# A load buffer more in the two MLPs of a decoder trunk, paid for with smaller operand tiles

## The chip, the cores and the metric

One NeuronCore of a Trainium2 chip runs the whole program. It has TensorE (matrix products), VectorE, ScalarE, GpSimd (its queue is called POOL here) and SyncE (SP), which only issues DMAs. The metric is the device time of one execution in microseconds.

## The reference, cut to what matters

Two pre-norm residual layers over 256 positions of width 2048. The mixers (attention of four kinds) stay as they are here. The change lies in the MLP that follows each mixer, with 8192 hidden columns:

```python
def squared_relu_mlp(h, w_up, w_down):
    return jnp.square(jax.nn.relu(h @ w_up)) @ w_down

for layer in range(DEPTH):                      # DEPTH = 2
    ...                                         # x = x + mixer(rms_norm(x))
    h = rms_norm(x, mlp_norm[layer])
    x = x + squared_relu_mlp(h, w_up[layer], w_down[layer])
```

All is float32; `w_up` and `w_down` are 64 MB each per layer, and every weight is read from memory once.

## The kernel before, in words

**Split operands.** Every float32 operand is split into a high part in TensorE's reduced format (`hi`) and the remainder (`lo`), and a product is made of hi·hi, hi·lo and lo·hi. For the weights this is done on the fly: a load brings 1 MB into a tile `raw` of 128 × 2048 (8 KB a partition), ScalarE copies 1024 columns of it into `hi` (L1317), VectorE subtracts to give `lo` (L1328), and TensorE uses both.

**One stream.** The whole kernel is a list `stream` of chunks (1024 weight columns a partition each), in the order in which TensorE consumes them. Chunks belong to load units (`Unit`), one DMA each on SP's queue. The main loop at the end of `trunk` makes, for chunk `i`, the `hi` of the chunks up to `i + 5` (`hi_to`, five buffers), the `lo` of those up to `i + 4` (`lo_to`, four buffers), and then the matmuls of chunk `i` (`chunk`). When the last chunk of a unit has its `lo`, `load_to` issues the next load. There are three `raw` buffers (`RAW_BUFS`), so a load waits until the unit three before it has been read.

**The MLP.** The hidden columns are cut into eight groups of 1024. `up_list(grp)` makes the group's hidden values in four blocks `b` of 256 columns (16 matmul steps each, into one PSUM pair called `up` or `s`); `up_done` evicts a block (ScalarE `t` L1002, VectorE L1003, ScalarE L1004 and L1008 into `hr`) and a job turns `hr` into the operand tile `hs`. For the first six groups the second matrix is applied with a fast scheme for 2 × 2 blocks (seven products in place of eight), for which `hs` holds seven combinations, each as hi and lo: a tile of 7 × 256. The pair `b = 3`, the one listed in `PLAIN`, goes the plain way with eight products and fills only four rows of its tile. `product_list(grp)` covers the output columns in four column blocks `cb`, with two load units of `w_down` each; `prep13` and `prep24` (L1062 to L1070) make the weights' combinations `w13` and `w24`. Products of group `grp` and up blocks of group `grp + 1` are interleaved by a fixed pattern in `mlp`: two chunks of products, one of up, and so on, so that a column block's seven chunks go with four chunks of up, and the loads come as w_down, w_up, w_down, w_up.

At the end of a column block ScalarE copies the two halves of its sums into `stage` tiles (L1118, two buffers), and POOL's queue stores them to `sums` in DRAM: the first group plainly (L1121), the others with an adding DMA (L1123). After the last of the six groups `combine` makes the outputs from `sums` by further adding DMAs (L1135) and copies (L1140), while TensorE goes on with the up blocks of the last group and then with the second matrix for the last two groups in the ordinary way ("down" blocks).

**Pools.** Each mixer and each MLP opens a memory pool of its own when its first chunk is reached and closes it when the next begins (`open_pool`, `pool_ctx.close`); the pools of successive phases use the same memory. The `raw`, `hi` and `lo` buffers are in a pool of their own (`wts`) that lasts throughout. The first five units go to tiles borrowed from the first mixer (`early`).

Of the kernel before, what the change touches and what calls it, by code (L numbers as in the profile page):

```python
# [10 lines left out]
F32 = mybir.dt.float32  # L11
F32R = mybir.dt.float32r
# [5 lines left out]
P = 128  # L18
# [20 lines left out]
RAW_BUFS, HI_BUFS, LO_BUFS = 3, 5, 4  # L39
# [6 lines left out]
class Jobs:  # L46


    def __init__(self, budget):
        self.t, self.budget = 0, budget  # L50
        self.jobs, self.done, self.owner = [], set(), {}
# [16 lines left out]
    def need(self, key):  # L68
        rounds = 0
        while key not in self.done:  # L70
            last = self.owner[key]
            for job in list(self.jobs):
                if job in self.jobs and not job[3]:
                    self.step(job)
                if key in self.done or job is last and rounds < 8:
                    break
            rounds += 1
# [33 lines left out]
class Unit:  # L111


    def __init__(self, load):
        self.load, self.users, self.raw = load, 0, None


class Chunk:
# [20 lines left out]
def trunk(ctx, tc, x, attn_norm, mlp_norm, w_up, w_down, ev_w_in, ev_q_norm, ev_w_uq, ev_kv_norm,  # L139
          ev_w_ukv, ev_w_out, od_w_in, od_sinks, od_w_out, final_norm, c_perm, c_rope, c_dist, out):  # L140
    nc = tc.nc
    wts = ctx.enter_context(tc.tile_pool(name="wts", bufs=1))
# [13 lines left out]
    def f32(ap):  # L156
        return ap.bitcast(F32)
# [4 lines left out]
    def temp():  # L162
        return tmp.tile([P, 2, T], F32, name="t", bufs=3)

    def split_into(dst, src, scale=1.0):

        act(dst[:, :, 0:T], src, AF.Copy, scale=scale)
        tt(dst[:, :, T:], src, f32(dst[:, :, 0:T]), op=OP.subtract)
# [3 lines left out]
    xin, early = [], []  # L172
# [21 lines left out]
    st = {}  # L194

    def open_banks(pool_ctx, name):
        st["banks"] = pool_ctx.enter_context(
            tc.tile_pool(name=name, bufs=1, space=bass.MemoryType.PSUM, reuse_waits="tile"))
# [228 lines left out]
    stream = []  # L427
# [535 lines left out]
    def mlp(layer, last):  # L963
# [4 lines left out]
        E = {}  # L968

        def open_pool():  # L970
            open_banks(pool_ctx, f"mlp{layer}_ps")
            E["pool"] = pool_ctx.enter_context(tc.tile_pool(name=f"mlp{layer}", bufs=1, reuse_waits="tile"))

        def load_gain():
            fn = [E["pool"].tile([P, D // 2], F32, name=n) for n in ("w13", "w24")]
            for i in range(2):
                c = slice(i * D // 2, (i + 1) * D // 2)
                nc.gpsimd.dma_start(fn[i], final_norm[c].unsqueeze(0).to_broadcast([P, D // 2]))
            E["fn"] = lambda c0, n: fn[c0 // (D // 2)][:, c0 % (D // 2):c0 % (D // 2) + n]

        NGRP, NS = 8, 6
        PLAIN = (3,)
        W = FF // NGRP
        nb = W // T
        up, down = w_up[layer], w_down[layer]
        sums = [dram.tile([P, 8 * T], F32, name=f"sums{layer}_{cb}") for cb in range(4)]
        hs = {}
# [11 lines left out]
        def up_done(grp, b):  # L999
            def f(ps):  # L1000
                t = temp()
                act(t, ps[:, :, T:], AF.Copy)  # L1002
                tt(t, ps[:, :, 0:T], t, op=OP.add)  # L1003
                act(t, t, AF.Relu)  # L1004
                if (grp, b) != (0, 0):
                    need(("h", layer) + ((grp, b - 1) if b else (grp - 1, nb - 1)))
                r = E["pool"].tile([P, 8, P], F32, name="hr", bufs=1)
                act(r[:, 0:4].rearrange("p (j k) t -> p j (k t)", j=2), t, AF.Square)  # L1008

                def job():  # L1010
                    h = E["pool"].tile([P, 7, 2 * P], F32R, name="hs", bufs=2 * nb)
                    if grp >= NS:
                        h = h.rearrange("p o t -> p (o t)")[:, 0:4 * T].rearrange("p (j t) -> p j t", j=2)
                        split_into(h, r[:, 0:4].rearrange("p (j k) t -> p j (k t)", j=2))
                    elif b in PLAIN:
                        act(h[:, 0:4, 0:P], r[:, 0:4], AF.Copy)
                        yield 1, 0
                        tt(h[:, 0:4, P:], r[:, 0:4], f32(h[:, 0:4, 0:P]), op=OP.subtract)
                    else:

                        tt(r[:, 4], r[:, 0], r[:, 2], op=OP.add)
                        tt(r[:, 6], r[:, 1], r[:, 0], op=OP.subtract)
                        tt(r[:, 5], r[:, 4], r[:, 1], op=OP.subtract)
                        tt(r[:, 7], r[:, 3], r[:, 5], op=OP.subtract)
                        yield 1, 0
                        act(h[:, :, 0:P], r[:, 1:8], AF.Copy)
                        yield 1, 0
                        tt(h[:, :, P:], r[:, 1:8], f32(h[:, :, 0:P]), op=OP.subtract)
                    hs[grp, b] = h
                    jobs.done.add(("h", layer, grp, b))  # L1030
                    yield 1, 0
                jobs.spawn(job(), keys=[("h", layer, grp, b)], delay=1)
            return f

# [166 lines left out]
        for grp in range(NS):  # L1201
            s, u = product_list(grp), up_list(grp + 1)
            for i in range(len(u)):
                a, b = (i // 4 * 7 + (0, 2, 4, 5, 7)[i % 4 + e] for e in range(2))
# [10 lines left out]
        for b in range(8):  # L1215
# [3 lines left out]
            else:  # L1219
                add(Block("T", w, h_mov, down_done(b), take=take_free(b), extra=add_sums(b)))  # L1220
        return open_pool, pool_ctx.close


# [63 lines left out]
    for f in (even_mixer, lambda: mlp(0, False), odd_mixer, lambda: mlp(1, True)):  # L1287
        a = len(stream)
        phases.append((a,) + tuple(f()))
    starts = {p[0]: i for i, p in enumerate(phases)}  # L1290
    total = len(stream)
    his, los = {}, {}
    units = []
    for block, c in stream:
        if block.chunks[c].unit not in units[-2:]:
            units.append(block.chunks[c].unit)
    at = {"load": 0, "free": 0, "hi": 0, "lo": 0}

    def load_to(n):
        while at["load"] < min(n, len(units)):  # L1300
            unit = units[at["load"]]
            n = at["load"]
            unit.raw = early[n] if n < len(early) else wts.tile([P, 2048], F32, name="raw", bufs=RAW_BUFS)
            unit.load(unit.raw)
            at["load"] += 1

    def views(i, dst):
        block, c = stream[i]
        chunk = block.chunks[c]
        return chunk.views(chunk.unit.raw, dst)  # L1310

    def hi_to(n):
        while at["hi"] < min(n, total):
            i = at["hi"]
            his[i] = wts.tile([P, 1024], F32R, name="hi", bufs=HI_BUFS)
            for d, r in views(i, his[i]):
                act(d, r, AF.Copy)  # L1317
            prep = stream[i][0].chunks[stream[i][1]].prep
            if prep:
                prep()  # L1320
            at["hi"] += 1

    def lo_to(n):
        while at["lo"] < min(n, total):
            i = at["lo"]
            los[i] = wts.tile([P, 1024], F32R, name="lo", bufs=LO_BUFS)
            for (d, r), (h, _) in zip(views(i, los[i]), views(i, his[i])):
                tt(d, r, f32(h), op=OP.subtract)  # L1328
            at["lo"] += 1
            unit = stream[i][0].chunks[stream[i][1]].unit  # L1330
            unit.users -= 1
            if unit.users == 0:
                at["free"] += 1
                load_to(max(at["free"], len(early)) + RAW_BUFS)

    def split_to(n):
        hi_to(n)
        lo_to(n)

    def chunk(i):  # L1340
        block, c = stream[i]
        consume(block, c, his.pop(i), los.pop(i))
# [49 lines left out]
    for b, n in enumerate((1, 2, 3, 3, 5, 5, 6, 6)):  # L1392
        load_x(b)
        load_to(n)
    load_to(7)
    x_turn(0)
    gains(g_first, 16, 0)
# [27 lines left out]
    for i in range(START, total):  # L1425
        if i in starts:
            phases[starts[i] - 1][2]()
            phases[starts[i]][1]()
        hi_to(i + HI_BUFS)
        lo_to(i + LO_BUFS)  # L1430
        chunk(i)
        block, c = stream[i]
        if block.tiles * len(block.chunks[c].kts) == 8 or block.kind == "S" and c in (1, 3, 4, 6):
            jobs.tick()
# [44 lines left out]
```

## Time and profile before

| | |
|---|---|
| median of three runs | 2197.22 us (2196.88 to 2203.35) |
| the profiled execution | 2204.07 us, of which the span of its instructions is 2202.3 us |
| TensorE matmul busy | 2159.3 us, 98% of the span |
| VectorE, ScalarE, POOL busy | 1588.7, 1284.6, 162.6 us |
| mean granted TensorE clock | 0.996 |
| DMA traffic | 459.43 MB, 209 GB/s over the span |
| loads of `w_up` | 128 of 1024 KB, 5.8 us from issue to landing in the median |

The page gives busy times and shares over the whole span, a chain of waits, groups of instructions and DMA issues; answers of the trace give single stretches. `L1317` is line 1317 of the kernel. "Idle before" an instruction is time in which its engine did nothing, and the name behind the arrow is what ended it. The first MLP occupies about 360 to 1090 us of the span, the second about 1460 us to the end.

### The profile page before, as it was taken

The page shows a single profiled execution, that of the slowest core. Times are in us where ns is not written, and L with a number is a line of the kernel's source. Part 1 is how long each engine was busy: PE and PEld are TensorE (multiplying, and loading weights), DVE is VectorE, ACT ScalarE, POOL GpSimd, SP SyncE. Part 2 cuts the span into 40 slices and gives each one's busy share as a digit, 9 for nine tenths or more (in the row PEclk, how much of TensorE's full clock was granted, in tenths as well). Part 3 has the DMA queues.
Part 4 walks back from the last instruction along what each step waited for, and adds up shares of the span by engine and source line. Part 5 has one row for each costly group of instructions (what it writes and reads, how often), then busy time and mean ns, then how long its engine had stood idle before and what let it go on. Part 6 is the DMA issues. An engine that isn't in the chain of part 4 may idle for free.

```text
span 2202.3 us, 35006 instructions
## 1 busy us (share of the span) xinstructions
PE 2159.3 (98%) x14038; PEld 1953.4 (89%) x14038; DVE 1588.7 (72%) x2120; ACT 1284.6 (58%) x1777; POOL 162.6 (7%) x217
## 2 busy tenths in 40 slices
PE   9999999999999999999999999999999999999998
PEld 7898988999999889878888889889999898988887
DVE  6765666788888778747766665567887887876476
ACT  6554545667666666555545446456766666665552
POOL 0000000000000000321000000000000000003210
PEclk9999999999999999999999999999999999999999
DMA  8545456578888879897654456566878888888973
GB/s 261 178 149 163 149 177 191 191 246 233 240 238 238 235 217 250 233 271 213 195 172 137 153 172 183 147 186 195 263 222 242 226 243 234 238 241 219 284 208 112
DMA packets 313811, 459.43 MB, mean 209 GB/s; under 512 B 11864, under 2 KB 198304, under 8 KB 313648
## 3 DMA queue, kind: packets, MB, share of 16 engines
q1 hardware_dynamic: 288416, 392.32, 56.5%
q0 software_dynamic: 25200, 64.86, 15.0%
q8 instruction: 110, 1.80, 0.3%
q14 instruction: 53, 0.43, 0.1%
q10 hardware_dynamic: 32, 0.01, 0.0%
HBM read 404.73 MB, written 60.82 MB: 211 GB/s over the span
## 4 chain that ended last, share of the span: by engine, by line
PE 58%; issue 22%; DMA 13%; DVE 3%; POOL 2%; ACT 2%; SPq 0%; POOLq 0%; ACTq 0%; DVEq 0%
PE mm L472 14%; PE mm L473 8%; DMA raw<-w_up 7%; PE s L472 6%; DMA sums<-sums 5%; PE up L472 5%; PE s L473 3%; PE up L473 3%; DVE lo L1328 2%; PE s L493 2%; PE s L494 2%; PE s L495 2%; PE mm L461 2%; PE mm L463 2%; PE mm L462 2%
## 5 line engine op out<-in xcount | busy, mean ns | idle before, releaser
L1328 DVE TENSOR_TENSOR lo<-raw,hi 128x1024 fp32r<-128x1024 f32 (+2 forms) x804 | 851.2, 1082 | 269.0 <-ACT hi L1317 109.3
L1317 ACT ACTIVATE hi<-raw 128x1024 fp32r<-128x1024 f32 (+2 forms) x804 | 738.9, 942 | 506.5 <-DMA raw<-w_up 185.3
L472 PE MATMUL up<-xs,hi 128*128 128x512 f32 x1440 | 522.6, 399 | 11.1 <-DVE t L1003 6.9
L473 PE MATMUL up<-xs,lo 128*128 128x256 f32 x1536 | 428.1, 284 | 9.4 <-DVE lo L1328 8.2
L494 PE MATMUL s<-lo,hs 128*128 128x256 f32 x1392 | 390.6, 281 | 0.0
L493 PE MATMUL s<-hi,hs 128*128 128x256 f32 x1392 | 390.5, 281 | 0.0
L495 PE MATMUL s<-hi,hs 128*128 128x256 f32 x1392 | 390.3, 280 | 0.0
L472 PEld LDWEIGHTS up<-xs,hi 128*128 128x128 f32 x1440 | 271.8, 189 | 70.9 <-DVE t L1003 10.4
L472 PE MATMUL mm<-xs,hi 128*128 128x512 f32 x885 | 319.4, 401 | 0.0
L473 PEld LDWEIGHTS up<-xs,lo 128*128 128x128 f32 x1536 | 290.5, 189 | 22.2 <-DVE lo L1328 19.6
L493 PEld LDWEIGHTS s<-hi,hs 128*128 128x128 f32 x1392 | 262.3, 188 | 6.5
L494 PEld LDWEIGHTS s<-lo,hs 128*128 128x128 f32 x1392 | 261.8, 188 | 2.1
L495 PEld LDWEIGHTS s<-hi,hs 128*128 128x128 f32 x1392 | 262.4, 188 | 0.0
L473 PE MATMUL mm<-xs,lo 128*128 128x256 f32 x944 | 259.1, 280 | 0.2 <-DVE lo L1328 0.2
L1328 DVE TENSOR_TENSOR lo<-w,hi 128x1024 fp32r<-128x1024 f32 x144 | 175.7, 1220 | 56.7 <-ACT hi L1317 56.7
L472 PEld LDWEIGHTS mm<-xs,hi 128*128 128x128 f32 x885 | 166.0, 188 | 37.3
L473 PEld LDWEIGHTS mm<-xs,lo 128*128 128x128 f32 x944 | 177.3, 188 | 3.1 <-DVE lo L1328 0.5
L472 PE MATMUL s<-xs,hi 128*128 128x512 f32 x480 | 171.5, 398 | 8.3 <-ACT stage L1118 5.6
L1317 ACT ACTIVATE hi<-w 128x1024 fp32r<-128x1024 f32 x144 | 150.9, 1048 | 19.2 <-DVE w L1070 15.8
L472 PE MATMUL s<-hs,hi 128*128 128x512 f32 x450 | 161.0, 398 | 0.0
L473 PE MATMUL s<-xs,lo 128*128 128x256 f32 x512 | 141.5, 281 | 1.2 <-DVE lo L1328 1.2
L1118 ACT ACTIVATE stage<-s 128x1024 f32<-128x1024 f32 x96 | 97.8, 1018 | 58.6 <-PE s L495 56.4
(312 smaller groups left out, 3130.6 us busy)
## 6 DMA issues: line engine op xcount, KB each, us to landing
raw<-w_up SPq DMA_DIRECT2D x128, 1024.0 KB, 5.8
raw<-w_down SPq DMA_DIRECT2D x128, 1024.0 KB, 5.5
sums<-stage POOLq DMA_DIRECT2D x96, 512.0 KB, 8.5
raw<-od_w_in SPq DMA_DIRECT2D x36, 1024.0 KB, 5.1
raw<-ev_w_in SPq DMA_DIRECT2D x30, 1024.0 KB, 5.3
raw<-ev_w_out SPq DMA_DIRECT2D x16, 1024.0 KB, 5.1
raw<-od_w_in SPq DMA_DIRECT2D x20, 512.0 KB, 4.9
sums<-sums POOLq DMA_DIRECT2D x64, 128.0 KB, 7.0
```

The lines of the kernel that those rows point to most:

```text
L461: mm(o, xh, hi[:, n], start=first, stop=False)
L462: mm(o, xh, lo[:, n], start=False, stop=False)
L463: mm(o, xl, hi[:, n], start=False, stop=last)
L472: mm(ps[:, j], hi[:, n, c], m, start=first, stop=False)
L473: mm(ps[:, j, 0:T], lo[:, n, c], m[:, 0:T], start=False, stop=False)
L493: mm(ps, x[:, a, 0:P], hi[:, w], start=(i, o) == bank[0], stop=False)
L494: mm(ps, x[:, a, 0:P], lo[:, w], start=False, stop=False)
L495: mm(ps, x[:, a, P:], hi[:, w], start=False, stop=(i, o) == bank[-1])
L1118: act(stage, ps.rearrange("p b c -> p (b c)"), AF.Copy)
L1317: act(d, r, AF.Copy)
L1328: tt(d, r, f32(h), op=OP.subtract)
```

## The change

Two things are done together. While an MLP runs, a fourth load buffer `raw` is taken from the MLP's own pool. The three buffers in `wts` become three tokens `None` in a list `spare`, and the fourth is a token with the number of its phase, added when the MLP's pool has been opened; every load takes the first token of the list, every unit that has been read gives its token back at the end of the list, and a token of a phase that the next unit no longer belongs to is thrown away. The fourth buffer takes 8 KB a partition. The operand tiles of the pair in `PLAIN` get a name and a size of their own (`hp`, 4 × 256 in place of 7 × 256, two tiles), and six tiles `hs` are left of eight, which is 6 KB a partition less.

```diff
 class Unit:
     def __init__(self, load):
-        self.load, self.users, self.raw = load, 0, None
+        self.load, self.users, self.raw, self.slot = load, 0, None, "early"
...
         def open_pool():
             open_banks(pool_ctx, f"mlp{layer}_ps")
             E["pool"] = pool_ctx.enter_context(tc.tile_pool(name=f"mlp{layer}", bufs=1, reuse_waits="tile"))
+            st["own_raw"] = lambda: E["pool"].tile([P, 2048], F32, name="raw")
...
                 def job():
-                    h = E["pool"].tile([P, 7, 2 * P], F32R, name="hs", bufs=2 * nb)
+                    if b in PLAIN:
+                        h = E["pool"].tile([P, 4, 2 * P], F32R, name="hp", bufs=2 * len(PLAIN))
+                    else:
+                        h = E["pool"].tile([P, 7, 2 * P], F32R, name="hs", bufs=2 * (nb - len(PLAIN)))
...
-    for block, c in stream:
-        if block.chunks[c].unit not in units[-2:]:
-            units.append(block.chunks[c].unit)
-    at = {"load": 0, "free": 0, "hi": 0, "lo": 0}
+    for i, (block, c) in enumerate(stream):
+        unit = block.chunks[c].unit
+        if unit not in units[-2:]:
+            unit.phase = sum(a <= i for a in starts) - 1
+            units.append(unit)
+    at = {"load": 0, "hi": 0, "lo": 0}
+
+    spare = [None] * RAW_BUFS
 
     def load_to(n):
         while at["load"] < min(n, len(units)):
             unit = units[at["load"]]
-            n = at["load"]
-            unit.raw = early[n] if n < len(early) else wts.tile([P, 2048], F32, name="raw", bufs=RAW_BUFS)
+            n_early = at["load"] < len(early)
+            if not n_early:
+                if spare and spare[0] not in (None, unit.phase):
+                    spare.pop(0)
+                if not spare:
+                    return
+                unit.slot = spare.pop(0)
+            if n_early:
+                unit.raw = early[at["load"]]
+            elif unit.slot is None:
+                unit.raw = wts.tile([P, 2048], F32, name="raw", bufs=RAW_BUFS)
+            else:
+                unit.raw = st["own_raw"]()
             unit.load(unit.raw)
             at["load"] += 1
...
             if unit.users == 0:
-                at["free"] += 1
-                load_to(max(at["free"], len(early)) + RAW_BUFS)
+                if unit.slot != "early":
+                    spare.append(unit.slot)
+                load_to(len(units))
...
         if i in starts:
             phases[starts[i] - 1][2]()
+            st.pop("own_raw", None)
             phases[starts[i]][1]()
+            if "own_raw" in st:
+                spare.append(starts[i])
+                load_to(len(units))
```

## The prediction

> **What bounds the kernel now.** I read the page first, then the waits of TensorE, of ScalarE and of the load queue, then three timelines, then the windows. Page, parts 1 and 6:
>
> ```profile
> span 2202.3 us, 35006 instructions
> ...
> PE 2159.3 (98%) x14038; PEld 1953.4 (89%) x14038; DVE 1588.7 (72%) x2120; ACT 1284.6 (58%) x1777; POOL 162.6 (7%) x217
> ...
> raw<-w_up SPq DMA_DIRECT2D x128, 1024.0 KB, 5.8
> ...
> sums<-stage POOLq DMA_DIRECT2D x96, 512.0 KB, 8.5
> ```
>
> TensorE is the bound: no other engine comes near 98%. A load buffer takes no matmul away, so all that can be won is time in which TensorE stands still or runs slowly. Its idle time seems to be only 2202.3 − 2159.3 = 43 us, start and end included; but the page says that matmul ends are modelled, so a stop shorter than one matmul hides in "busy". I therefore measure the loss by the beat of the work. In the MLPs every column block of the second matrix (`cb`, four a group, six groups) ends with the same two issues to `sums` on POOL's queue. Timeline of POOL, first issue of each column block (first MLP, then the second):
>
> ```profile
> 425.52 0.59 POOL L1121 DMA_DIRECT2D sums<-stage  x1 [331.75 <-ACT stage L1118]
> ...
> 511.77 0.90 POOL L1123 DMA_DIRECT2D sums<-stage  x1 [19.18 <-ACT stage L1118]
> ...
> 533.33 0.86 POOL L1123 DMA_DIRECT2D sums<-stage  x1 [18.83 <-ACT stage L1118]
> ...
> 643.81 0.86 POOL L1123 DMA_DIRECT2D sums<-stage  x1 [18.52 <-ACT stage L1118]
> ...
> 666.52 0.86 POOL L1123 DMA_DIRECT2D sums<-stage  x1 [18.18 <-ACT stage L1118]
> ...
> 869.39 0.86 POOL L1123 DMA_DIRECT2D sums<-stage  x1 [18.33 <-ACT stage L1118]
> ...
> 1524.10 0.59 POOL L1121 DMA_DIRECT2D sums<-stage  x1 [427.90 <-ACT stage L1118]
> ...
> 1966.62 0.86 POOL L1123 DMA_DIRECT2D sums<-stage  x1 [18.25 <-ACT stage L1118]
> ```
>
> From 425.52 to 511.77 lie four column blocks: 86.25 / 4 = 21.56 us each, and 511.77 to 533.33 is 21.56 again. That is the beat when nothing is late. From 643.81 to 666.52 it is 22.71. The twenty blocks from 425.52 to 869.39 take 443.87 us where 20 × 21.56 = 431.2 would do: 12.7 us lost. The twenty from 1524.10 to 1966.62 take 442.52: 11.3 us lost. Together 24.0.
>
> Who is late? Waits of TensorE, of ScalarE and VectorE, and of the load queue (SPq):
>
> ```profile
> PE up L473 <- DVE lo L1328: 8.2, 9, 3.3
> PE up L472 <- DVE t L1003: 6.9, 14, 1.0
> PE s L472 <- ACT stage L1118: 5.6, 2, 4.2
> PE up L472 <- ACT hi L1317: 4.1, 2, 2.7
> ...
> ACT hi L1317 <- DMA raw<-w_up: 185.3, 75, 11.0
> DVE lo L1328 <- ACT hi L1317: 167.2, 115, 9.9
> ...
> SPq L1179 <- DVE lo L1328: 727.9, 160, 11.8
> SPq L1041 <- DVE lo L1328: 587.1, 96, 10.7
> ```
>
> TensorE waits for what VectorE and ScalarE make; those wait for `hi`; `hi` waits 185.3 us for loads of `w_up`; and the queue that issues the MLP loads waits 727.9 + 587.1 us for `lo` to have read a buffer. So these loads are late because they start late, for want of a buffer.
>
> **The change, part by part.** *The buffer.* Four loads are made per column block. Timeline of the load queue over one beat, and two of these loads in the chain of waits (start, duration):
>
> ```profile
> 655.58 0.37 SPq L1041 DMA_DIRECT2D raw<-w_down  x1
> 662.47 0.37 SPq L1179 DMA_DIRECT2D raw<-w_up  x1
> 666.00 0.37 SPq L1041 DMA_DIRECT2D raw<-w_down  x1
> 669.06 0.37 SPq L1179 DMA_DIRECT2D raw<-w_up  x1
> 677.47 0.37 SPq L1041 DMA_DIRECT2D raw<-w_down  x1
> 684.09 0.37 SPq L1179 DMA_DIRECT2D raw<-w_up  x1
> 687.62 0.37 SPq L1041 DMA_DIRECT2D raw<-w_down  x1
> ...
> 662.47 5.48 DMA raw<-w_up
> ...
> 690.69 10.76 DMA raw<-w_up
> ```
>
> With three buffers a buffer's turn is from one load to the third after it: 655.58 to 669.06, 662.47 to 677.47, 666.00 to 684.09, 669.06 to 687.62, or 13.5, 15.0, 18.1, 18.6, mean 16.3. The beat allows 21.56 × 3/4 = 16.2. The turn just fails, which is why the first MLP holds the beat for some blocks and then falls behind as its reserve is used up. With four buffers the beat allows 21.56: 5.3 us of room in each turn. Each load is issued at the release before its own (the one of 662.47 at 655.58, that of 669.06 at 666.00), on average 21.56/4 = 5.4 us earlier.
>
> What the lateness does in one beat, ScalarE's timeline:
>
> ```profile
> 668.03 1.06 ACT L1317 ACTIVATE hi<-raw 128x1024 fp32r<-128x1024 f32 x1 [1.80 <-DMA raw<-w_up]
> 669.00 1.01 ACT L1118 ACTIVATE stage<-s 128x1024 f32<-128x1024 f32 x1
> 669.90 1.05 ACT L1317 ACTIVATE hi<-w 128x1024 fp32r<-128x1024 f32 x1
> 670.85 0.59 ACT L1002 ACTIVATE t<-up 128x512 f32<-128x512 f32 x1
> ```
>
> ScalarE stands 1.80 us before a `hi` whose load (662.47 + 5.48) has just landed; the two evictions queued behind it, `stage` and `t`, go late, and TensorE cannot start the next up block in their one bank. The 14 waits on `t` are thus mostly the load's as well. A load 5.4 us earlier covers 1.80. A window in which the beat held (length, then busy time of PE, PEld, DVE, ACT, POOL, then TensorE's granted clock, DMA share, GB/s):
>
> ```profile
> 500.00:550.00 50.00, 50.00 (x351) 46.59 (x350) 41.46 (x56) 34.13 (x42) 3.49 (x4) 1.00 0.84 232
> ```
>
> Next late after that is nothing that I can find: the same instructions ran here in the same order with TensorE busy throughout and VectorE at 41.46 of 50 us. I take 22 of the 24.0 us; ends 0 (the load is not the cause) and 24.0.
>
> *The change of groups.* After the last products, the `combine` copies on POOL's queue and the loads share the DMA engines. Windows, same columns:
>
> ```profile
> 900.00:950.00 50.00, 44.76 (x290) 40.23 (x289) 27.50 (x32) 22.08 (x28) 14.04 (x19) 0.97 0.92 237
> 950.00:1000.00 50.00, 48.23 (x271) 41.42 (x272) 29.79 (x30) 32.56 (x42) 17.18 (x23) 1.00 1.02 269
> 2000.00:2050.00 50.00, 41.21 (x255) 36.72 (x254) 26.46 (x31) 23.34 (x29) 15.76 (x22) 0.93 0.90 230
> ...
> 915.00:920.00 5.00, 3.79 (x13) 3.30 (x14) 4.97 (x7) 4.20 (x5) 1.65 (x2) 0.66 0.78 145
> ...
> 2025.00:2030.00 5.00, 4.92 (x37) 4.42 (x36) 4.72 (x7) 3.57 (x6) 3.30 (x5) 1.00 0.40 49
> 2030.00:2040.00 10.00, 10.00 (x74) 9.43 (x73) 4.56 (x6) 2.01 (x2) 3.23 (x5) 1.00 1.00 211
> ```
>
> Idle here: 5.24 + 1.77 + 8.79 = 15.8 us. The clock costs 0.03 × 50 + 0.07 × 50 = 5.0 more. Together 20.8. Before the worst stop the DMA engines stand at 0.40 (2025 to 2030: all three buffers are full) and then run at 1.00 without catching up; a fourth buffer would have used that hole. But inside the crowd an earlier issue only waits longer. Ends: 0, if the crowd decides, and 20.8, if the earlier start does. I take half, 10, since one hole stands against one crowded stretch.
>
> At 915 to 920, right after TensorE's longest wait on `lo` (3.3 us), the clock is at 0.66. The Trainium skill, TensorE: Matmul & The Clock Gate, Part 1: The HAM clock gate, says that an idle window of about 3.4 us sends the clock to half rate, and that shorter gaps don't. By that rule halving the stops would bring back all of the 5.0, and the gain here would be 7.9 + 5.0 = 12.9 and not 10; the trace shows the drop, not how short a stop must be to avoid it.
>
> *The room.* The operand tile of the fourth pair goes from `hs` (7 rows) to `hp` (4 rows), two tiles of it and six of `hs` in place of eight. Each turn stays two groups long, the same instructions write and read the same elements, so no wait is added: 0, covered by the beat at 21.56, which held with the same turn. If a turn did shorten, the next group's `act` into it would stop ScalarE; nothing in the code does that.
>
> *The start of each MLP.* One more load goes out when the pool opens. It is queued on SP behind loads already issued; what waits behind it is only the next load, which needs a release some microseconds later. Its memory is that of the mixer's first tiles, last read in the attention, before the output projection. 0; if it had to wait for the projection's end, one load would be late by a few microseconds, once per MLP, within the range.
>
> *The rule for issuing.* Outside the MLPs `load_to` has the same three tokens in the same order: 0. When units of the next mixer come up the fourth token is dropped: 0.
>
> Sum: 22 + 10 = 32 us. The profiled execution took 2204.07 (span 2202.3 and 1.8 around it): 2172. The median of the three runs shown is 2197.22, 6.85 lower. If those 6.85 are fewer stops, only 44.8 − 6.9 = 38 us are there to win and the share of 32/44.8 gives 27: 2170; if not, 2197 − 32 = 2165. I say 2168.
>
> **Rivals.**
> 1. *The DMA engines decide.* For it: shares of 1.00 at 2030 and 1.02 at 950. Against it in the products: 0.84 at full beat. Then the group changes win nothing and the products half to all of theirs: 12 to 24 us, 2173 to 2185. The Trainium skill, DMA: Bandwidth & Descriptors, Queues, rings and completion order, says that each DMA engine takes turns between the queues that have work, packet by packet; so a second load waiting in the same queue gets no larger share beside POOL's copies. The trace does not show the turns themselves.
> 2. *The load is not the cause, or the buffer comes to nothing.* If ScalarE's order (`stage`, `hi`, `t`) makes the stops by itself, TensorE's waits on `t` stay, and the fourth load only sits longer. Against it: the five beats from 425.52 to 533.33 ran in that order without loss. Gain 0 to 6: 2191 to 2197.
> 3. *Slower: POOL's stores starve.* `stage` has two buffers; each must be stored before its next use, 21.56 us later. The store takes 8.5 us in the median; it would have to pass 19.7 (beat less the issue of 0.86 and the eviction of 1.01) to decide. Each microsecond above costs TensorE one, in up to 40 blocks: at 20.7 us some 40 us, 2237. Loads ask for the same bytes per beat as before, which speaks against it.
>
> **How the numbers follow.** Forecast (both terms in good part, 2152 to 2175): 0.68. Rival 1: 0.20. Rival 2: 0.07. Rival 3: 0.05. The lower end takes the whole pool, 2197 − 45 = 2152; the upper must reach into rival 1 and past it until at most 2 in 10 is out: 2188. A measurement here tells 0.3%, 6.6 us, from no change. Forecast and rival 1 are faster by more than that: 0.88; rival 2 within it: 0.07; rival 3 slower: 0.05.
>
> **What would show it.** Right: the POOL issues at 21.56 us through all six groups; ScalarE's wait on `raw<-w_up` from 185.3 to under 60; loads landing later after their issue than 5.8 us, as two are under way; the windows of the group change at a clock of 1.00. Wrong: beats of 22 and more with `hi` waiting for loads issued long before (rival 1), or with no such wait (rival 2); `stage` waiting for `sums` (rival 3).

## The result, and the profile after

The changed kernel takes 2162.59 us in the median (2159.46 to 2164.85) against 2198.73 (2196.88 to 2203.35) of the kernel before in the same comparison: 36.1 us less, a ratio of 0.9832 with a 95% interval of 0.9811 to 0.9852. Compared once more, beside the last experiments, it was 0.9820 (0.9801 to 0.9840). The forecast was 2168, in a range of 2152 to 2188.

The page of the kernel after, parts 1 and 6:

```profile
span 2160.3 us, 35009 instructions
...
PE 2141.6 (99%) x14038; PEld 1949.6 (90%) x14038; DVE 1588.6 (74%) x2120; ACT 1290.0 (60%) x1777; POOL 163.1 (8%) x217
...
raw<-w_up SPq DMA_DIRECT2D x128, 1024.0 KB, 5.6
```

The span is 42.0 us shorter than before; the profiled execution of before (2204.07) lay above its timed runs, which is the difference to 36.1. VectorE and ScalarE are busy about as long as before (1588.6 and 1290.0 us) in a shorter span.

POOL's timeline, first store of a column block (`sums<-stage`; L1121 and L1123 have become L1125 and L1127):

```profile
425.72 0.59 POOL L1125 DMA_DIRECT2D sums<-stage  x1 [331.42 <-ACT stage L1122]
...
641.31 0.87 POOL L1127 DMA_DIRECT2D sums<-stage  x1 [18.83 <-ACT stage L1122]
...
662.87 0.86 POOL L1127 DMA_DIRECT2D sums<-stage  x1 [18.83 <-ACT stage L1122]
...
856.91 0.86 POOL L1127 DMA_DIRECT2D sums<-stage  x1 [18.83 <-ACT stage L1122]
...
1503.51 0.59 POOL L1125 DMA_DIRECT2D sums<-stage  x1 [428.63 <-ACT stage L1122]
...
1934.70 0.86 POOL L1127 DMA_DIRECT2D sums<-stage  x1 [18.84 <-ACT stage L1122]
```

Twenty blocks take 856.91 − 425.72 = 431.19 us in the first MLP and 1934.70 − 1503.51 = 431.19 in the second: the beat of 21.56 throughout (641.31 to 662.87 as well, where it was 22.71). That is 12.7 and 11.3 us less than before, 24.0 together. The other 18.0 of the 42.0 lie behind these blocks.

Waits of the kernel after, of ScalarE and TensorE:

```profile
ACT stage L1122 <- DMA sums<-stage: 13.8, 4, 6.0
...
PE s L472 <- ACT stage L1122: 3.8, 2, 2.1
...
ACT hi L1336 <- DMA raw<-w_up: 1.7, 3, 1.1
```

ScalarE's wait for loads of `w_up` has gone from 185.3 us to 1.7. Beside 1.6 us at the start of the second MLP, as before, TensorE has two stops left in the MLPs, and they have another cause: a `stage` tile whose store has not landed. ScalarE's timeline and the windows show the place (columns as in the prediction's windows):

```profile
925.14 1.03 ACT L1122 ACTIVATE stage<-s 128x1024 f32<-128x1024 f32 x1 [5.68 <-DMA sums<-stage]
...
2003.28 1.03 ACT L1122 ACTIVATE stage<-s 128x1024 f32<-128x1024 f32 x1 [6.04 <-DMA sums<-stage]
```

```profile
900.00:950.00 50.00, 48.27 (x303) 43.12 (x302) 29.07 (x31) 30.95 (x38) 14.52 (x20) 1.00 0.98 264
950.00:1000.00 50.00, 50.00 (x290) 43.68 (x290) 32.32 (x39) 28.59 (x37) 14.21 (x20) 1.00 0.95 252
...
2000.00:2050.00 50.00, 47.91 (x265) 41.45 (x264) 25.19 (x25) 29.41 (x36) 16.80 (x24) 0.97 1.05 290
```

The idle time in these three windows is 1.73 + 0 + 2.09 = 3.8 us, where it was 15.8, and the lowered clock costs 0.03 × 50 = 1.5 us, where it was 5.0. That is 15.5 of the 18.0; the rest is not located.

### The profile page after: what moved, and what is told of

Same layout as the page of the kernel before. It is cut to its first block, busy times and chain, and to the rows that moved or that the text cites. A ratio compares the mean times of both kernels' runs of the same rounds, so it can differ in the third digit from the quotient of the medians.

```text
span 2160.3 us, 35009 instructions
## 1 busy us (share of the span) xinstructions
PE 2141.6 (99%) x14038; PEld 1949.6 (90%) x14038; DVE 1588.6 (74%) x2120; ACT 1290.0 (60%) x1777; POOL 163.1 (8%) x217
## 4 chain that ended last, share of the span: by engine, by line
PE 49%; issue 39%; DMA 8%; POOL 4%; ACT 0%; POOLq 0%; SPq 0%; DVE 0%; ACTq 0%
PE mm L472 15%; PE mm L473 8%; PE s L472 6%; DMA sums<-sums 6%; PE s L473 4%; POOL sums L1127 3%; PE mm L461 2%; PE mm L463 2%; PE mm L462 2%; PE up L472 1%; DMA sums<-stage 1%; PE mm L475 1%; PE side L352 1%; PE up L473 1%; PE s L495 1%
## 5 line engine op out<-in xcount | busy, mean ns | idle before, releaser
L472 PE MATMUL up<-xs,hi 128*128 128x512 f32 x1440 | 516.6, 396 | 0.0
L473 PE MATMUL up<-xs,lo 128*128 128x256 f32 x1536 | 423.5, 281 | 0.0
L494 PE MATMUL s<-lo,hs 128*128 128x256 f32 x1008 | 282.9, 281 | 0.0
L493 PE MATMUL s<-hi,hs 128*128 128x256 f32 x1008 | 282.9, 281 | 0.0
L495 PE MATMUL s<-hi,hs 128*128 128x256 f32 x1008 | 282.7, 280 | 0.0
L493 PEld LDWEIGHTS s<-hi,hs 128*128 128x128 f32 x1008 | 189.9, 188 | 6.5
L494 PEld LDWEIGHTS s<-lo,hs 128*128 128x128 f32 x1008 | 189.7, 188 | 2.1
L495 PEld LDWEIGHTS s<-hi,hs 128*128 128x128 f32 x1008 | 190.0, 189 | 0.0
L472 PE MATMUL s<-hs,hi 128*128 128x512 f32 x360 | 129.9, 399 | 0.0
```

The costliest lines, as they stand in the source:

```text
L472: mm(ps[:, j], hi[:, n, c], m, start=first, stop=False)
L473: mm(ps[:, j, 0:T], lo[:, n, c], m[:, 0:T], start=False, stop=False)
L493: mm(ps, x[:, a, 0:P], hi[:, w], start=(i, o) == bank[0], stop=False)
L494: mm(ps, x[:, a, 0:P], lo[:, w], start=False, stop=False)
L495: mm(ps, x[:, a, P:], hi[:, w], start=False, stop=(i, o) == bank[-1])
```

## The experiments

The theory at the start was the prediction's: with three buffers a buffer's turn (load plus hold) is a little too long for the beat. The rivals: the new layout of the tiles does it; any reserve of 8 KB would do; the DMA engines decide.

### The smaller operand tiles alone

```diff
-                    h = E["pool"].tile([P, 7, 2 * P], F32R, name="hs", bufs=2 * nb)
+                    if b in PLAIN:
+                        h = E["pool"].tile([P, 4, 2 * P], F32R, name="hp", bufs=2 * len(PLAIN))
+                    else:
+                        h = E["pool"].tile([P, 7, 2 * P], F32R, name="hs", bufs=2 * (nb - len(PLAIN)))
```

> The smaller operand tiles (hp and hs) alone, with three load buffers as before. Theory (the fourth buffer makes the whole gain): the same time as before, 2198.7 within 6 us, and beats of the column blocks that lose 10 to 13 us over twenty blocks in each MLP, as before. Rival (the new layout of the operand tiles or of the pool removes waits): part of the 36 us, so 2190 or less, with beats nearer to 21.56.

Measured: 2199.06 us, ratio 0.9999 (0.9984 to 1.0013). Its twenty blocks, POOL's timeline:

```profile
425.95 0.59 POOL L1124 DMA_DIRECT2D sums<-stage  x1 [331.75 <-ACT stage L1121]
...
866.01 0.86 POOL L1126 DMA_DIRECT2D sums<-stage  x1 [18.25 <-ACT stage L1121]
...
1522.48 0.59 POOL L1124 DMA_DIRECT2D sums<-stage  x1 [428.30 <-ACT stage L1121]
...
1963.11 0.86 POOL L1126 DMA_DIRECT2D sums<-stage  x1 [18.31 <-ACT stage L1121]
```

440.06 and 440.63 us: 8.9 and 9.4 us lost, a little less than the 10 to 13 expected, at the same time in all. The smaller tiles only make room. The room is needed: without them the MLP's pool would take 92 KB a partition of the 87.25 that are left, so the fourth buffer alone was not tried.

### The fourth buffer in the first MLP only

```diff
+            if layer == 0:
                 st["own_raw"] = lambda: E["pool"].tile([P, 2048], F32, name="raw")
```

> The whole change, but the fourth buffer only in the first MLP; the second runs with three. Theory (each MLP's stops are its own): the first MLP as in the changed kernel, twenty beats in 431.2 us, the second as before, twenty beats in some 442; time about 2198.7 - 18 = 2181 (2176 to 2186). Rival (work that arrives earlier in one MLP carries a reserve through the next mixer, or the gain hangs on both): the second MLP changes too, and the time is under 2174 or over 2190.

Measured: 2181.20 us, ratio 0.9914 (0.9890 to 0.9938).

```profile
426.20 0.59 POOL L1126 DMA_DIRECT2D sums<-stage  x1 [331.76 <-ACT stage L1123]
...
857.40 0.86 POOL L1128 DMA_DIRECT2D sums<-stage  x1 [18.84 <-ACT stage L1123]
...
1503.88 0.59 POOL L1126 DMA_DIRECT2D sums<-stage  x1 [428.17 <-ACT stage L1123]
...
1948.63 0.86 POOL L1128 DMA_DIRECT2D sums<-stage  x1 [19.21 <-ACT stage L1123]
```

431.20 us in the first MLP, 444.75 in the second. About half the gain, and in the MLP that has the buffer; the second loses 13.6 us in its twenty blocks, so nothing is carried through the mixer.

### Two load buffers

```diff
-RAW_BUFS, HI_BUFS, LO_BUFS = 3, 5, 4
+RAW_BUFS, HI_BUFS, LO_BUFS = 2, 5, 4
```

> The kernel before with two load buffers throughout, mixers too. Read by the beats of the MLPs, since the mixers change as well. Theory (the turn of a buffer sets the beat when it is longer than the beat allows): with two buffers the beat allows 10.8 us a turn; a turn of at least 7.2 us of load and some 4 us of reading is 11 or more, so the beat is at least 22 and, since the hold can not shrink all the way, 23 to 27 us in the first group already. Rival (the engines, not the turn, make the stops): 22.1 us in the mean as with three.

Measured: 2825.21 us in one run. POOL's timeline, four blocks:

```profile
434.90 0.59 POOL L1121 DMA_DIRECT2D sums<-stage  x1 [340.78 <-ACT stage L1118]
...
575.85 0.90 POOL L1123 DMA_DIRECT2D sums<-stage  x1 [24.94 <-ACT stage L1118]
```

The beat is 35.2 us, far over the 23 to 27 expected. So the number of load buffers does set the beat where it is short, but the price was not what a sum of load and reading gave: a turn is here 35.2 / 2 = 17.6 us, longer than with three buffers. The loads took 6.5 us in the median from 600 to 1200 us, so the hold (the rest of the turn) did not shrink when time was short. It contains waits of engines on each other, and the clock, granted at 0.85 to 0.88 from 500 to 800 us, stretches it too; it can't be put together from durations of instructions.

### The stores without the adding

```diff
-                if grp == 0:
+                if True:
                     nc.gpsimd.dma_start(to, stage)
```

> The kernel before (three load buffers), with every group's sums stored plainly over the last ones, as the first group's are: the adding in the stores is left out. Theory (an adding store stretches the one load per beat that goes beside it from about 8.5 to about 11.7 us, and the reserve of three buffers doesn't cover that): beats of 21.56 through all twenty blocks, 22 to 24 us gained in the products, the change of groups as before; about 2176. Rival (the reserve fails by itself, whatever the stores do): beats fall behind after some blocks as before, 2190 to 2200.

This kernel leaves out the summing over groups, so its output is not the reference's; only its time is of use. Measured: 2162.89 us, ratio 0.9831 (0.9810 to 0.9852): with three buffers the time of the changed kernel.

```profile
425.79 0.59 POOL L1121 DMA_DIRECT2D sums<-stage  x1 [331.75 <-ACT stage L1118]
...
856.99 0.53 POOL L1121 DMA_DIRECT2D sums<-stage  x1 [19.17 <-ACT stage L1118]
```

Twenty blocks in 431.20 us, and in the second MLP 1938.91 − 1507.72 = 431.19. How long the loads of the stretch from 600 us to the twentieth block take, from issue to landing, in the kernel before, this one, and the kernel after, in this order:

```profile
DMA to landing us min/median/max: 5.0/5.8/14.3
```

```profile
DMA to landing us min/median/max: 4.9/5.4/8.6
```

```profile
DMA to landing us min/median/max: 4.9/5.5/12.3
```

The late load is the one that is issued just behind the first adding store of a column block. In the kernel before that is one load of `w_up` per block, issued 1.2 to 2.5 us behind the store: it takes 10.6 to 14.3 us in this stretch, every other load 8.9 or less. In the kernel after it is a load of `w_down`, and two blocks show how much the order counts; the first stores of these blocks go out at 641.31 and 684.44 us:

```profile
L1045 SPq DMA_DIRECT2D raw<-w_down x1: 368/368/368, 641.8 to 641.8; - x1
...
DMA to landing us min/median/max: 12.3/12.3/12.3
...
L1045 SPq DMA_DIRECT2D raw<-w_down x1: 368/368/368, 683.8 to 683.8; - x1
...
DMA to landing us min/median/max: 5.8/5.8/5.8
```

Issued 0.5 us behind the store the load takes 12.3 us; issued 0.65 us ahead of it, 5.8. Without the adding, a load 0.5 us behind the store takes 7.1 to 8.6 us, and three buffers cover that. With a fourth buffer the long load is still there, and no longer matters. Of the 37 us gained in the medians some 13 lie at the change of groups, which was not expected. It may come from reaching that place with a full reserve, or from the last group's own stores, which are plain there too; no run separates the two.

### Without combine's adding copies, three buffers and four

```diff
-                for to, src in step:
-                    nc.gpsimd.dma_start(to, src, accum_op=OP.add)
                 yield 2, 0
```

Three buffers:

> The kernel before (three load buffers) without the adding copies of combine (the last copies from the sums stay): the sums are read as they are. Theory (the stops at the change of groups need both a short reserve and the crowd of copies; without the crowd three buffers do): the idle time there, 7 us in the first MLP and 8.8 in the second, and the low clock go, the beats of the products stay as they are; about 2178. Rival (three buffers are short there whatever POOL does): 2190 or more.

Four:

> The changed kernel without the adding copies of combine. Theory (what is left at the change of groups is the store of a stage tile that is queued on POOL behind the copies and lands late): ScalarE's 13.8 us of waits for stage go, TensorE's two stops of 2 us and the clock after the second go; 4 to 6 us, about 2157. Rival (what is left are late loads): no change, 2162.

Both kernels leave out `combine`'s adding, so their outputs are not the reference's; only their times are of use. Measured: three buffers 2182.73 us, ratio 0.9923 (0.9905 to 0.9941); four buffers 2156.37 us, 0.9804 (0.9786 to 0.9821). With three the stops at the change of groups go, but for 2.2 us of idle time in the three windows, and the beats stay bad (440.8 and 441.5 us for twenty blocks). With four TensorE has no stop left in either MLP but the 1.6 us at the start of the second. The changed kernel was measured at 2162.59 and 2160.58 in two other comparisons, so the crowd of copies still costs it 4 to 6 us; with three buffers the same crowd cost some 17 (2200.20 of the kernel before in this comparison less 2182.73).

### The steps of the copies further apart

```diff
                 for to, src in step:
                     nc.gpsimd.dma_start(to, src, accum_op=OP.add)
-                yield 2, 0
+                yield 4, 0
```

> The changed kernel with the four steps of combine four ticks apart in place of two; nothing is left out. Theory (POOL's queue stands at a step's copies because the step before has not landed, and the stage store behind it goes late): the stores go out in time, the two stops of 2 us shrink, 2156 to 2160. Rival (the copies are wanted by the down blocks, or the crowd only moves): same time or some us slower, 2162 to 2170.

Measured: 2167.22 us, ratio 0.9859 (0.9838 to 0.9881), 5 to 7 us more than the changed kernel; the rival's time. Its waits:

```profile
ACT hi L1336 <- DMA raw<-w_up: 46.0, 13, 7.7
...
PE up L472 <- ACT hi L1336: 2.0, 1, 2.0
```

No wait of ScalarE for a `stage` tile is listed any more, but loads of `w_up` are late in its stead, from 915 to 962 us and from 1995 to 2043. The edit did not spread the copies, though. `combine` runs per column block and starts while the last group's other blocks are still at work. With its steps further apart, the steps of two blocks alternate on POOL's queue, which then waits less for the copy before. These are POOL's wait and the last copies in the first MLP, of the changed kernel and then of this one:

```profile
POOL sums L1139 <- DMA sums<-sums: 106.3, 27, 8.4
...
993.20 1.11 POOL L1144 DMA_DIRECT2D stage<-sums  x2 [5.37 <-DMA sums<-sums]
```

```profile
POOL sums L1139 <- DMA sums<-sums: 61.3, 25, 6.2
...
969.21 1.11 POOL L1144 DMA_DIRECT2D stage<-sums  x2 [5.13 <-DMA sums<-sums]
```

Both begin at about 866 us, so the crowd became shorter and denser: the DMA share from 900 to 950 us is 1.10 in place of 0.98. The slower time is a result about a denser crowd; whether a thinner one would help was not tested.

### The same 8 KB for hi and lo

```diff
-        hi_to(i + HI_BUFS)
-        lo_to(i + LO_BUFS)
+        hi_to(ahead(i, HI_BUFS))      # i + 6 inside an MLP
+        lo_to(ahead(i, LO_BUFS))      # i + 5 inside an MLP
```

A sixth `hi` and a fifth `lo` tile come from the MLP's own pool; three load buffers, operand tiles as in the change.

> The same 8 KB a partition spent elsewhere: smaller operand tiles, three load buffers, and in the MLPs a sixth hi and a fifth lo buffer in the MLP's own pool, with hi and lo made one chunk further ahead. Theory (a load buffer's turn, load plus hold, is what fails by 0.1 us in 16.2): a chunk of reserve is half a load unit; the turn does not get shorter by much, so the beats still lose a good part, 2180 to 2195. Rival (any reserve between the loads and TensorE would do): the time of the changed kernel, 2160 to 2167, and twenty beats in 431.2.

Measured: 2177.16 us, ratio 0.9904 (0.9877 to 0.9932). The time lies between the two ranges, 3 us below the theory's; the beats are the rival's: 430.4 us for twenty blocks in both MLPs. The theory of the turn fell here: three load buffers hold the beat if the splitting is further ahead. What is lost is lost at the changes of groups. Waits of TensorE, and ScalarE's timeline there:

```profile
PE s L472 <- ACT stage L1122: 14.8, 2, 8.0
```

```profile
930.69 1.06 ACT L1333 ACTIVATE hi<-raw 128x1024 fp32r<-128x1024 f32 x1 [12.48 <-DMA raw<-w_up]
931.66 1.00 ACT L1122 ACTIVATE stage<-s 128x1024 f32<-128x1024 f32 x1
```

ScalarE works in program order. It waits 12.48 us for a load, with the eviction of `s` queued behind; TensorE stops for the eviction, 6.8 us here and 8.0 in the second MLP. The kernel before has the same sequence once: ScalarE waits 11.04 us for a load until 2043.38, and TensorE stops 4.2 us. So late loads at this place come with three load buffers, and one chunk more of `hi` ahead of the eviction goes with longer stops; that it is the reason for their length is argued.

### Only lo further ahead

```diff
         hi_to(i + HI_BUFS)
-        lo_to(i + LO_BUFS)
+        lo_to(ahead(i, LO_BUFS))      # i + 5 inside an MLP
```

Here the theory was a new one: loads start earlier because `lo` reads the buffer earlier.

> Three load buffers, smaller operand tiles, and in the MLPs only a fifth lo buffer (4 KB), with lo made one chunk earlier; hi as before. Theory now (a load can start only when lo has read the buffer three units before, and lo is tied to TensorE by its buffers; so an earlier lo is an earlier load, with no more of hi queued ahead of the evictions on ScalarE): loads go out some 2 us earlier in the beat and clear of the second store, their longest falls from 11.5 to some 7 us, twenty beats in 431.2, and ScalarE has no 12 us waits at the change of groups; 2168 to 2178. Rival (it was the sixth hi buffer that helped): beats fall behind as before, 2190 and more.

Measured: 2190.19 us, ratio 0.9961 (0.9944 to 0.9978); the new theory fell as well. Twenty blocks take 439.59 and 437.46 us. TensorE's waits:

```profile
PE up L472 <- DVE t L1004: 20.3, 21, 3.7
```

The longest load from 600 us on took 11.4 us here, and 7.3 with `hi` and `lo` both ahead:

```profile
DMA to landing us min/median/max: 5.0/6.3/11.4
```

```profile
DMA to landing us min/median/max: 5.0/5.6/7.3
```

With both ahead the load nearest to the stores goes out 1.0 to 2.0 us ahead of the first one and takes 6.3 to 6.9 us, adding or not; with `lo` alone it goes out 1.3 to 3.1 us behind it and takes 10.2 to 11.4, and VectorE's eviction `t` goes late. Why the pattern of the loads settles on the one side of the store in one kernel and on the other side in the other is open. `hi` alone further ahead has no time: in that order the program waits for itself and never ends.

### A better kernel: the last block's sums go to idle tiles

```diff
-                stage = E["pool"].tile([P, 4 * T], F32, name="stage", bufs=2)
+                if grp == NS - 1 and cb == 3:
+                    stage = E["pool"].tile([P, 4 * T], F32, name="w13" if half == "s0" else "w24")
+                else:
+                    stage = E["pool"].tile([P, 4 * T], F32, name="stage", bufs=2)
```

Run beside the changed kernel itself, and beside the same edit on the kernel with only `lo` ahead.

> The changed kernel once more, beside the three others: 0.983 of the kernel before, twenty beats in 431.2 us in both MLPs, two stops of some 2 us at the changes of groups.

> The changed kernel, and the last column block of the last group of products is copied out to the tiles w13 and w24, which are idle by then, and not to the two stage tiles. Theory (what is left is ScalarE waiting for a stage tile whose store lands late): the waits for stage at that block go, and with them the two stops; 4 to 6 us below the changed kernel, 2157 or 0.980 to 0.981 of the kernel before. Rival (the loads behind are as late, as when the copies were spread): within 3 us of the changed kernel.

> The one with the fifth lo buffer and the last block's copies to w13 and w24. Theory (at the change of groups late loads decide with three load buffers, and the stage tiles only with four): within 4 us of the one with the fifth lo buffer alone. Rival (the stage tiles decide there as well): 5 us and more below it.

Measured: the changed kernel 2160.58 us (2159.88 to 2163.04, five runs), with one stop of 2.1 us where two were expected; with this edit 2157.01 (2156.17 to 2157.84, five runs), ratio to the kernel before 0.9802 (0.9783 to 0.9821). The two sets of runs don't overlap; 3.6 us between the medians, a little under the 4 to 6 expected. ScalarE's waits for `stage` tiles are gone, and so are the stops; windows of this kernel at the changes of groups:

```profile
900.00:950.00 50.00, 50.00 (x317) 44.93 (x316) 30.47 (x32) 32.50 (x42) 16.06 (x24) 1.00 1.02 276
...
2000.00:2050.00 50.00, 50.00 (x286) 43.60 (x285) 26.17 (x27) 29.67 (x39) 14.04 (x20) 1.00 1.09 309
```

It is within 1 us of the kernel with four buffers and no adding copies at all (2156.37), so little is left of what the crowd costs. On the kernel with only `lo` ahead the same edit does nothing: 2193.50 us, 0.9959 (0.9944 to 0.9973). The stage tiles gained time only where the loads were no longer late.

## Why the prediction was right, point by point

**The bound and the pool to win.** Right. TensorE's lost time in the products, measured by the beat, was 24.0 us, and all of it came back.

**The cause.** Right as far as it said that loads were late and a fourth buffer would cover it: the smaller tiles alone give nothing, the buffer in one MLP gives half, and ScalarE's wait for `w_up` went from 185.3 to 1.7 us.

**The turn of 16.3 us against 16.2.** Wrong as an argument. In a steady run with three buffers and four loads a beat the mean turn is 3/4 of the beat, whatever makes the beat late; a beat of 21.7 gives 16.3. The figure restated the loss and did not explain it. The experiments showed it: three buffers hold the beat when the stores don't add, or when `hi` and `lo` are further ahead, and with two buffers the turn is 17.6, so it is no fixed price. What the runs showed in its place: one load per beat goes out just behind an adding store and takes 10.6 to 14.3 us in place of 7.1 to 9.6 without the adding (both MLPs), and three buffers lack the time for it. The good beats at the start were read as a reserve that is used up; it was passed over that the first four blocks are stored plainly. The adding starts at 511.77 us, and the first late beat ends at 577.80. That the forecast held in spite of this is in part luck: its size came from the measured beat, and a fourth buffer covers a late load whatever makes it late.

**The products, 22 us of 24.0.** 24.0 measured. Nothing was late next.

**The change of groups, 10 us of 20.8.** The mis-sized term: 15.5 of the 20.8 came back, and 2.5 more outside these windows or hidden in them. Half was chosen because an early load would wait in the crowd. But with the fourth buffer the waiting there cost little: without the copies only 4 to 6 us more are gained. Of the clock's 5.0 us 3.5 came back; the rest is the stop of 2.09 us, behind which the clock fell to 0.57.

**The room, the start of each MLP, the mixers.** Nothing, as predicted, as far as the runs show it: 0.9999 for the tiles alone, and the first store of the first MLP goes out at 425.72 us in place of 425.52.

**The sum.** 32 us forecast, 42.0 in the profiled executions and 36.1 in the medians.

**The signs to look for.** The beat and ScalarE's wait: as said. The clock: 1.00 in the first MLP, 0.97 in the second. Loads landing later after their issue than 5.8 us: wrong, 5.6.

**The rivals.** DMA engines as the bound: not in the products, and 4 to 6 us at the change of groups, of which 3.6 were a matter of two tiles. POOL's stores did become the next wait, as `stage` waiting for `sums`, but only at two places, as what is left and not as a slowdown.

## What to carry to other kernels

Measure the loss of a pipelined engine by the beat of its work and compare with the beat where nothing is late: TensorE's visible idle time fell by 24.3 us (2202.3 − 2159.3 less 2160.3 − 2141.6) while 42.0 were won. A mean turn of a buffer taken from a steady run is the beat in other words and proves nothing about its cause; take away the transfer that is suspected, or add a buffer in one of two places. Ask what queues behind a reserve: the same 8 KB gave 2162.59 us as a load buffer and 2177.16 as a further chunk of `hi` and `lo`, where evictions stood behind a `hi` that waited for its load.

## What the runs showed of the hardware that was not expected

A stop of 2 us was followed by a lower clock. In the kernel after, TensorE stopped for 2.09 us until 2004.36 and for 1.73 us until 926.22. The granted clock (third figure from the end) behind the one and the other:

```profile
2004.00:2008.00 4.00, 3.64 (x12) 3.10 (x13) 1.23 (x1) 2.90 (x4) 0.00 (x0) 0.57 1.12 311
...
926.00:930.00 4.00, 3.78 (x21) 3.33 (x22) 1.23 (x1) 3.00 (x5) 0.00 (x0) 1.00 1.12 254
```

0.57 after the first and 1.00 after the second. The traces of the other runs with three or four load buffers agree. Behind all 17 stops of 2.03 to 8.0 us (the first 20 us of the span left out) the clock was 0.50 to 0.68 over the next 4 us, behind all 22 of 1.24 to 1.60 it was 1.00, and behind the five between, 1.69 to 1.90, it was lowered three times. The Trainium skill, TensorE: Matmul & The Clock Gate, Part 1: The HAM clock gate, speaks of an idle window of about 3.4 us; here stops a good deal shorter were enough, so the rule's gap is not a safe one.

And the price of an adding store for the load beside it hangs on which goes out first. From 600 us to the twentieth block of the kernel after, 1 MB loads that took 5.5 us in the median took 11.2 to 12.3 when issued 0.5 us behind the first of two adding stores of 512 KB, and 5.6 to 5.8 when issued 0.65 us ahead of it. Behind plain stores of the same size, with three buffers, it was 7.1 to 8.6.
